# Tied tiles, later remainders, a regrouped conditioning and one root at the end of a decoder step

## The chip, the cores and the metric

The kernel runs on one core of a Trainium2 chip. The metric is the device time of one execution in microseconds (us), the median of the runs. TensorE (PE) multiplies, VectorE (DVE), ScalarE (ACT) and GpSimd (POOL) work on elements, and SyncE (SP) issues most transfers.

## The reference

One layer of a decoder, for a prompt of 512 tokens and a group of 8 sample tokens with their states, at width 1024, in float32:

```
mod = silu(c) @ w_mod + b_mod                  # six parts: shift, scale, gate, twice
h   = rmsnorm(x) * (1 + scale1) + shift1
u   = h @ w_in                                 # 8 column blocks of 1024
o_a = HGRN2 heads of (q, f, i, gate)           # 8 heads, chunked recurrence
o_b = RG-LRU(conv(x_b)) * gelu(y_b)
merged = sigmoid(g_a) * (o_a @ w_branch_a) + sigmoid(g_b) * (o_b @ w_branch_b)
x   = x + gate1 * (merged @ w_out)
h2  = rmsnorm(x) * (1 + scale2) + shift2
x   = x + gate2 * (square(relu(h2 @ w_ff1)) @ w_ff2)
y   = rmsnorm(x) * final_norm_g
```

The outputs are `y_prompt` (512 x 1024), `y_sample` (8 x 1024) and the states after the step.

## The kernel before

Activations lie transposed: 128 features on the partitions, 512 + 8 tokens along the free axis, cut into two halves of 260. Every float32 operand is split in two (a rounded part `whi` or `hi`, and the remainder `wlo` or `lo`), and a product is three matrix products: `whi` x `hi`, `whi` x `lo`, `wlo` x `hi`. A plain tile (`gemm`) makes 128 output features out of 1024: eight blocks k of 128 inputs, three products, two halves, so 48 matmuls. They are issued by `products` (L157), block after block, all three products of a block together.

The weights of a tile are loaded by SP into one of four buffers, the pool `wst` (L104), cast by ACT to `whi` (L114), and the remainder is made by DVE (`wlo`, L118). There are two places for such pairs in this part of the program, so the cast of a tile begins when the tile two before it is done. The loads stand in the order of `weights`: at most `LOADS` = 3 ahead of the splitting, all on SP's queue, each waiting for its buffer.

A scheduler places the instructions on the engines: it goes by the program's data and by priorities (`urgent` lifts an instruction ahead), unless `behind` ties one instruction after another without a wait. In `gemm`, `after` is such a tie for the `whi` products. Before the change it is set only after a conditioning step (`rows_last`), so products of neighbouring tiles may mix.

The conditioning `mod` is computed in pieces. Of its six parts two are made at the start, the other four as eight steps between other work. A step (`mod`, `mod_rows` L362) is 32 matmuls of four loaded rows of `w_mod`, 512 KB each; these rows go through the same four `wst` buffers, but are used as they are, unsplit, and hold their buffer until the step. Four steps stand among the gate products, one at each of four groups, two in the branch tiles (after b3 and a3, set by `share` and `due`), two after the w_out tiles 1 and 4.

The stages: heads, RG-LRU and first gates up to about 430 us, the second gates (`gate_product`, L916, weights `wgate`) up to 482, the branch tiles b0 to b7 and a0 to a7, w_out, then a feed-forward part with a plan of its own.

At the end, the last two of eight feature blocks of x (blocks 6 and 7) get their last products. `final_pair(2, 1)` transposes blocks 4 and 5 of the last token quarters and the samples: ACT squares the result with a running sum (`fss`), DVE multiplies it by `final_norm_g` into `fx` (rows) and `fxs` (samples; in the trace it is part of the tile `fin`). `last_transposes` does the same for blocks 6 and 7 by a product with `gdiag`, `last_squares` squares their x on ACT (`snap`), `last_sums` adds the squares up over the partitions in PSUM, on top of the reduced `fss` (`part`, from `last_parts`). `last_root` takes the square root (ACT) and the reciprocal (DVE), `row` multiplies one quarter of 128 tokens and sends it off, 768 columns and then 256. Quarters 0 and 1 are done earlier, in `last_half`. From (j = 4) on, PE, ACT and DVE work strictly in the order written (`InOrder`; all these instructions carry line 73).

Of the kernel before, what the change touches and what calls it, by code (L numbers as in the profile page):

```python
# [32 lines left out]
LOADS = 3  # L33
MODK = 7
ROWN = 4
FIRSTS = 3
# [44 lines left out]
class Kernel:  # L81
# [67 lines left out]

    def products(self, ps, w, a, first, last, extra=0, halves=(0, 1), after=None):  # L150

        (wh, wl), (ah, al) = w, a
        ps = ps if isinstance(ps, list) else [ps[:, 0], ps[:, 1]]
        for n, (x, y) in enumerate(((wh, ah), (wh, al), (wl, ah))):
            for s in halves:
                c = slice(s * HALF, (s + 1) * HALF + s * extra)
                self.last_product = self.nc.tensor.matmul(ps[s][:, :c.stop - c.start], x, y[:, c],  # L157
                                                          start=first and n == 0, stop=last and n == 2)
# [1266 lines left out]
    def final_pair(self, m, s):  # L1425
# [27 lines left out]
    def added_last(self, j, ps):  # L1453
# [10 lines left out]
        def add_samples(t, op=OP.add):  # L1464
            self.nc.vector.tensor_tensor(zs[t], zs[t], ps[:, n:], op)
# [5 lines left out]
        with self.urgent():  # L1471
# [21 lines left out]
            if j == 3:  # L1493
                self.last_rows = [self.pmm.tile([128, 2, 512], F32, name="mm")[:, 0],
                                  self.pps.tile([128, 512], F32, name="ps")]
                self.last_transposes(1, 1)
                self.last_sums(1, 1)
                add(0, g[0], True)
                add_samples(0)
                samples_done(self.nc.vector, 0)  # L1500
                self.last_squares(1, 0)
                self.last_sums(1, 0)
                self.last_transposes(1, 0)
                sq = self.sm.tile([128, 2, NB], F32, name="sqx")
                for t in (0, 1):
                    self.nc.vector.tensor_tensor(sq[:, t], x[t][:, L:], x[t][:, L:], OP.mult)
                self.last_root(self.fr[:, 2:4], self.sums[:, 1, :2])
                pt = self.ppt.tile([128, 512], F32, name="pt")
                for t in (0, 1):
# [5 lines left out]
                for t in (0, 1):  # L1515
                    self.nc.tensor.matmul(ss, sq[:, t], self.one, start=False, stop=True, skip_group_check=True)
                self.row(2, self.nc.vector)
                self.row(3, self.nc.scalar)
                self.row(2, self.nc.vector, self.last_rows[0])
                r = self.fr[:NB, NC:NC + 1]  # L1520
                self.last_root(r, ss)
                self.row(3, self.nc.scalar, self.last_rows[1])
                self.nc.vector.tensor_scalar(self.fxs[:, :768], self.fxs[:, :768], r, None, OP.mult)
                self.nc.vector.tensor_scalar(self.fxs[:, 768:], pt[:NB, :256], r, None, OP.mult)
                self.nc.scalar.dma_start(self.o["y_s"][:, 0], self.fxs)

    def last_half(self):

        with self.urgent():
# [8 lines left out]
            self.final_pair(2, 1)  # L1538
            self.last_parts(1)

# [15 lines left out]
    def last_sums(self, s, j):  # L1556

        ps = self.sums[:, s, :2]
        first = (s, 1 - j) not in self.summed
        self.summed.add((s, j))  # L1560
        if first:
            self.nc.tensor.matmul(ps, self.ident, self.part[:, 2 * s:2 * s + 2], start=True, stop=True,
                                  skip_group_check=True)
# [7 lines left out]

    def row(self, t, eng, p=None):

# [5 lines left out]
        else:  # L1579
            eng.tensor_scalar(y, src, r, None, OP.mult)  # L1580
        self.nc.sync.dma_start(self.o["y_p"][0, t * 128:(t + 1) * 128, c], y)

    def run(self):
# [508 lines left out]
```

## Time and profile before

| what | value |
|---|---|
| median of 3 runs | 1001.22 us (1001.22 to 1002.68) |
| profiled execution | 1001.28 us, its span 999.5 us |
| busy: PE, DVE, ACT, POOL | 98%, 69%, 52%, 14% of the span |
| matmuls | 9644 |
| granted clock of TensorE, mean | 0.996 |
| transferred | 143.67 MB |

The profile comes from one execution of the span given, 1.8 us shorter than the time of that run. The word that stands behind `<-` in a row of the timeline is what released the instruction, with the idle time of the engine ahead of it. Times in rows are microseconds from the start of the span.

### The profile page before, as it was taken

The page shows a single profiled execution, that of the slowest core. Times are in us where ns is not written, and L with a number is a line of the kernel's source. Part 1 is how long each engine was busy: PE and PEld are TensorE (multiplying, and loading weights), DVE is VectorE, ACT ScalarE, POOL GpSimd, SP SyncE. Part 2 cuts the span into 40 slices and gives each one's busy share as a digit, 9 for nine tenths or more (in the row PEclk, how much of TensorE's full clock was granted, in tenths as well). Part 3 has the DMA queues.
Part 4 walks back from the last instruction along what each step waited for, and adds up shares of the span by engine and source line. Part 5 has one row for each costly group of instructions (what it writes and reads, how often), then busy time and mean ns, then how long its engine had stood idle before and what let it go on. Part 6 is the DMA issues. An engine that isn't in the chain of part 4 may idle for free. (4 is left out here: it accounts for less than half of the span.)

```text
span 999.5 us, 23206 instructions
## 1 busy us (share of the span) xinstructions
PE 981.9 (98%) x9644; PEld 955.6 (96%) x9644; DVE 691.1 (69%) x1359; ACT 523.9 (52%) x996; POOL 135.1 (14%) x247
## 2 busy tenths in 40 slices
PE   8999999999999999999999999999999999999997
PEld 6899999999999999999889999999999999999996
DVE  7795866686596667887525557767677766768785
ACT  5565645735664572565412324566456555646663
POOL 1300000000000100121000000012311331232050
PEclk9999999999999999999999999999999999999998
DMA  9663253253334336357545646322752572272242
GB/s 348 238 200 122 95 166 125 81 170 108 111 117 137 127 100 210 112 183 272 192 159 183 209 161 222 116 83 61 190 147 69 112 191 79 71 185 62 64 85 86
DMA packets 48858, 143.67 MB, mean 144 GB/s; under 512 B 6241, under 2 KB 15905, under 8 KB 47721
## 3 DMA queue, kind: packets, MB, share of 16 engines
q1 hardware_dynamic: 37280, 123.47, 36.8%
q0 software_dynamic: 11456, 18.70, 8.5%
q8 instruction: 75, 1.23, 0.5%
q14 instruction: 31, 0.25, 0.1%
q10 hardware_dynamic: 16, 0.03, 0.0%
HBM read 123.65 MB, written 11.26 MB: 135 GB/s over the span
## 5 line engine op out<-in xcount | busy, mean ns | idle before, releaser
L157 PE MATMUL mm<-h,whi 128*128 128x260 f32 (+1 forms) x2720 | 450.8, 285 | 0.0
L157 PEld LDWEIGHTS mm<-h,whi 128*128 128x128 f32 x2720 | 377.7, 189 | 1.3 <-issue 0.2
L157 PE MATMUL mm<-h,wlo 128*128 128x260 f32 x1360 | 280.4, 285 | 0.4 <-DVE wlo L118 0.4
L118 DVE TENSOR_TENSOR wlo<-wst,whi 128x1024 fp32r<-128x1024 f32 x156 | 190.6, 1223 | 127.2 <-ACT whi L114 122.8
L114 ACT CAST whi<-wst 128x1024 fp32r<-128x1024 f32 x156 | 163.3, 1049 | 151.7 <-PE mm L157 101.4
L157 PEld LDWEIGHTS mm<-h,wlo 128*128 128x128 f32 x1360 | 212.8, 189 | 1.5 <-issue 0.6
L1299 POOL TENSOR_TENSOR ft<-ft,fsh 128x8 f32<-128x8 f32 x28 | 18.4, 658 | 209.1 <-DVE ft L1293 209.1
L1307 DVE TENSOR_TENSOR f<-f 128x260 f32<-128x260 f32 x64 | 27.4, 427 | 27.8 <-ACT f L1302 27.1
L1296 ACT ACTIVATE ft<-ft,fsh 128x512 f32<-128x512 f32 (+2 forms) x36 | 24.0, 676 | 36.1 <-DVE ft L1293 36.1
L157 PE MATMUL mm<-b,whi 128*128 128x260 f32 x256 | 41.4, 284 | 0.9 <-ACT whi L114 0.9
L157 PE MATMUL mm<-a,whi 128*128 128x260 f32 x256 | 41.3, 284 | 0.0
L234 POOL TENSOR_SCALAR ss<-ss 128x4 f32<-128x4 f32 x8 | 2.7, 334 | 285.2 <-ACT g L672 285.2
L157 PE MATMUL mm<-oa,whi 128*128 128x260 f32 x256 | 41.2, 283 | 0.0
L157 PEld LDWEIGHTS mm<-b,whi 128*128 128x128 f32 x256 | 35.1, 189 | 1.7 <-ACT whi L114 1.3
L588 DVE TENSOR_TENSOR X<-X,tb 128x512 f32<-128x512 f32 x48 | 31.0, 691 | 7.0 <-PE ps L576 3.7
L157 PEld LDWEIGHTS mm<-a,whi 128*128 128x128 f32 x256 | 35.0, 188 | 0.8 <-PE pt L362 0.4
L157 PEld LDWEIGHTS mm<-oa,whi 128*128 128x128 f32 x256 | 34.9, 188 | 0.4 <-issue 0.4
L1341 POOL DMA_DIRECT2D ma<-snap x28 | 26.4, 956 | 40.6 <-issue 32.3
L1323 POOL DMA_DIRECT2D ma<-snap x28 | 25.9, 926 | 38.5 <-DMA ma<-snap 23.5
L1302 ACT ACTIVATE f<-ft 128x520 f32<-128x520 f32 (+1 forms) x36 | 20.8, 587 | 15.0 <-POOL ft L1300 13.0
L182 ACT ACTIVATE gate<-pb,pa 128x260 f32<-128x260 f32 x32 | 15.5, 483 | 24.5 <-PE pb L720 24.5
L157 PE MATMUL mm<-b,wlo 128*128 128x260 f32 x128 | 25.9, 284 | 0.5 <-DVE wlo L118 0.5
(566 smaller groups left out, 2071.9 us busy)
## 6 DMA issues: line engine op xcount, KB each, us to landing
wst<-in_w_ff_dram SPq DMA_DIRECT2D x64, 512.0 KB, 4.4
wst<-in_w_in_dram SPq DMA_DIRECT2D x56, 512.0 KB, 3.8
wst<-in_w_mod_dram SPq DMA_DIRECT2D x32, 512.0 KB, 6.2
wm<-in_w_piece_dram SPq DMA_DIRECT2D x4, 1024.0 KB
wm<-in_w_rows_dram SPq DMA_DIRECT2D x4, 1024.0 KB, 11.8
st<-in_state_hgrn_dram SPq DMA_DIRECT2D x8, 512.0 KB
vb<-vd SPq DMA_DIRECT2D x8, 512.0 KB, 4.2
out_dram<-st SPq DMA_DIRECT2D x8, 512.0 KB, 3.7
```

The source lines that it names most:

```text
L114: ins = self.nc.scalar.copy(hi, st)
L118: self.nc.vector.tensor_tensor(lo, st, hi.bitcast(F32), OP.subtract)
L157: self.last_product = self.nc.tensor.matmul(ps[s][:, :c.stop - c.start], x, y[:, c], start=first and n == 0, stop=last and n == 2)
L182: ins = self.nc.scalar.activation(out, x, AF.Sigmoid, **kw)
L234: p.tensor_scalar(out, x, n * EPS, None, OP.add)
L588: last = nc.vector.tensor_tensor(half, half, factors(tbs, x, b), OP.mult)
L1296: nc.scalar.activation(t[:, :p], t[:, :p], AF.Relu, bias=sh[:, 0:1])
L1299: eng.tensor_tensor(t[:, p:], t[:, p:], sh[:, 1:9], OP.add)
L1302: nc.scalar.activation(f, self.two(self.ft)[:, a:a + n], AF.Square)
L1307: self.nc.vector.tensor_tensor(f[:, n], f[:, a], f[:, b], op)
L1323: nc.gpsimd.dma_start(x[1][:, b], v[:, :n], accum_op=OP.add)
L1341: nc.gpsimd.dma_start(x[t][:, a], s[p], accum_op=OP.add)
```

## The change

1. `gemm` ties its `whi` products after the product issued last (`self.last_product`) where there is no conditioning step to tie to.
2. `LATE = 4`: a tile first issues the two `whi` products of blocks 0 to 3 (16 matmuls), then their four `wlo` products (8 matmuls), then blocks 4 to 7 as before. The number of matmuls is the same.
3. The copy of the sample values in `head_sample_v` is urgent.
4. The eight conditioning steps stand in other places: three among the gate products (none at the last group), three in the branch tiles (after b4, a1 and a6), two after the w_out tiles 1 and 4.
5. `final_pair` issues DVE's products ahead of ACT's squares.
6. The end is rewritten: the sum of the samples' squares becomes a third column of the last sums, so that one root of 128 x 3 and one reciprocal serve rows and samples; the transposes stand ahead of the sums; the reduction stands behind the last additions; the samples' first 768 columns are multiplied by POOL; the second piece of row 3 leaves on ACT's queue, the samples on SP's; the PSUM tile for `last_rows[0]` comes from another pool.

```diff
+LATE = 4
@@ products
+            if n not in parts:
+                continue
@@ gemm
-        after, self.rows_last = after or self.rows_last, None
+        after, self.rows_last = after or self.rows_last or self.last_product, None
...
-                n = q * KO + k
-                self.products(ps, (hi[:, k], lo[:, k]), acts[n], n == 0, n == len(keys) * KO - 1, extra,
-                              after=after)
+                for j, parts in ((k, (0, 1, 2)),) if k >= LATE else \
+                        ((k, (0, 1)),) + tuple((j, (2,)) for j in range(LATE) if k == LATE - 1):
+                    n = q * KO + j
+                    self.products(ps, (hi[:, j], lo[:, j]), acts[n], n == 0, n == len(keys) * KO - 1, extra,
+                                  after=after, parts=parts)
@@ head_sample_v
-        nc.vector.tensor_copy(vs, ps[:NB, :128])
+        with self.urgent():
+            nc.vector.tensor_copy(vs, ps[:NB, :128])
@@ final_pair
+        if s:
+            nc.vector.tensor_tensor(self.fxs[:, fs], p2[:NB, :256], self.gbc[:NB, fs], OP.mult)
+        nc.vector.tensor_tensor(self.fx[:, 2 * s:2 * s + 2, fs], p.rearrange("p (t f) -> p t f", f=256),
+                                self.gbc[:, None, fs].to_broadcast([128, 2, 256]), OP.mult)
         for t in range(2):
             nc.scalar.activation(junk, p[:, 256 * t:256 * t + 256], AF.Square,
                                  accum_out=self.fss[:, 2 * s + t, m:m + 1])
         if s:
             nc.scalar.activation(junk[:NB], p2[:NB, :256], AF.Square, accum_out=self.fss[:NB, NC, m:m + 1])
-            nc.vector.tensor_tensor(self.fxs[:, fs], p2[:NB, :256], self.gbc[:NB, fs], OP.mult)
-        nc.vector.tensor_tensor(self.fx[:, 2 * s:2 * s + 2, fs], p.rearrange("p (t f) -> p t f", f=256),
-                                self.gbc[:, None, fs].to_broadcast([128, 2, 256]), OP.mult)
@@ added_last, j == 3
-                self.last_rows = [self.pmm.tile([128, 2, 512], F32, name="mm")[:, 0],
+                self.last_rows = [self.ppb.tile([128, 512], F32, name="pb"),
                                   self.pps.tile([128, 512], F32, name="ps")]
                 self.last_transposes(1, 1)
-                self.last_sums(1, 1)
                 add(0, g[0], True)
                 add_samples(0)
+                self.last_parts(1)
                 samples_done(self.nc.vector, 0)
                 self.last_squares(1, 0)
+                sq = ...                                  # the samples' squares, as before
+                self.last_transposes(1, 0)
+                self.last_sums(1, 1)
                 self.last_sums(1, 0)
-                self.last_transposes(1, 0)
-                self.last_root(self.fr[:, 2:4], self.sums[:, 1, :2])
+                for t in (1, 0):
+                    self.nc.tensor.matmul(self.sums[:NB, 1, 2:3], sq[:, t], self.one, start=False, stop=True,
+                                          skip_group_check=True)
                 pt = ...                                  # two products, as before
-                ss = self.sums[:NB, 0, 2:3]
-                self.nc.tensor.matmul(ss, self.ident[:, :NB], self.part[:, NC:NC + 1], start=True, stop=True,
-                                      skip_group_check=True)
-                for t in (0, 1):
-                    self.nc.tensor.matmul(ss, sq[:, t], self.one, start=False, stop=True, skip_group_check=True)
+                self.last_root(self.fr[:, 2:5], self.sums[:, 1, :3])
+                r = self.fr[:NB, NC:NC + 1]
+                self.nc.gpsimd.tensor_tensor(self.fxs[:, :768], self.fxs[:, :768], r.to_broadcast([NB, 768]), OP.mult)
                 self.row(2, self.nc.vector)
                 self.row(3, self.nc.scalar)
                 self.row(2, self.nc.vector, self.last_rows[0])
-                r = self.fr[:NB, NC:NC + 1]
-                self.last_root(r, ss)
-                self.row(3, self.nc.scalar, self.last_rows[1])
-                self.nc.vector.tensor_scalar(self.fxs[:, :768], self.fxs[:, :768], r, None, OP.mult)
+                self.row(3, self.nc.scalar, self.last_rows[1], self.nc.scalar)
                 self.nc.vector.tensor_scalar(self.fxs[:, 768:], pt[:NB, :256], r, None, OP.mult)
-                self.nc.scalar.dma_start(self.o["y_s"][:, 0], self.fxs)
+                self.nc.sync.dma_start(self.o["y_s"][:, 0], self.fxs)
@@ last_sums: slices 2 -> 2 + s, so that the samples' sums are the third column
@@ run
-        share, due = 1 / KO, 0.5
+        share, due = 3 / (2 * KO), 0.2
...
-            if j == 5:
+            if j == 5 and u < n - 1:
                 mod_step(1)
```

Three places in the order of the instructions. First TensorE between the branch tiles b2 and b3, before the change: `mm_6844` is b1, `mm_6903` b2, `mm_6959` b3; the `b_` names are the blocks of the activations.

```order
L157 MATMUL mm_6844<-b_6059,wlo_6725 128x260 x2
L157 MATMUL mm_6903<-b_6017,whi_6791 128x260 x2
L157 MATMUL mm_6903<-b_6018,whi_6791 128x260 x2
L157 MATMUL mm_6959<-b_6017,whi_6847 128x260 x2
L157 MATMUL mm_6959<-b_6018,whi_6847 128x260 x2
L157 MATMUL mm_6959<-b_6017,wlo_6848 128x260 x2
```

The same place after it: `mm_6872` is b2 and `mm_6928` b3.

```order
L160 MATMUL mm_6872<-b_6059,wlo_6761 128x260 x2
L160 MATMUL mm_6928<-b_6017,whi_6816 128x260 x2
L160 MATMUL mm_6928<-b_6018,whi_6816 128x260 x2
L160 MATMUL mm_6928<-b_6023,whi_6816 128x260 x2
L160 MATMUL mm_6928<-b_6024,whi_6816 128x260 x2
L160 MATMUL mm_6928<-b_6029,whi_6816 128x260 x2
L160 MATMUL mm_6928<-b_6030,whi_6816 128x260 x2
L160 MATMUL mm_6928<-b_6035,whi_6816 128x260 x2
L160 MATMUL mm_6928<-b_6036,whi_6816 128x260 x2
L160 MATMUL mm_6928<-b_6017,wlo_6817 128x260 x2
```

Before, b3 begins four products into b2 and takes the place of 25 products before b2 goes on; now b3 begins with b2 complete, and its first remainder stands behind 16 products. No two plain tiles are mixed any more.

Second, SP's queue of loads from the gates on, before and after:

```order
L104 DMA wst<-in_w_mod_dram 128x1024 x16
L104 DMA wst<-in_w_branch_b_dram 128x1024 x5
L104 DMA wst<-in_w_mod_dram 128x1024 x4
L104 DMA wst<-in_w_branch_b_dram 128x1024 x3
L104 DMA wst<-in_w_branch_a_dram 128x1024 x5
L1142 DMA wst<-in_w_ff_dram 128x1024 x4
```
```order
L105 DMA wst<-in_w_mod_dram 128x1024 x12
L105 DMA wst<-in_w_branch_b_dram 128x1024 x6
L105 DMA wst<-in_w_mod_dram 128x1024 x4
L105 DMA wst<-in_w_branch_b_dram 128x1024 x2
L105 DMA wst<-in_w_branch_a_dram 128x1024 x3
L105 DMA wst<-in_w_mod_dram 128x1024 x2
L1148 DMA wst<-in_w_ff_dram 128x1024 x4
L105 DMA wst<-in_w_mod_dram 128x1024 x2
```

Four rows of `w_mod` less stand ahead of the first branch weights, and two groups of four stand among the branch weights instead of one, the second of them around the first feed-forward loads.

Third, DVE at the end, from the last pair on, before and after:

```order
L73 TENSOR_TENSOR fin<-mm,fin 8x256
L73 TENSOR_TENSOR fx<-mm,fin 128x2x256
L73 TENSOR_REDUCE fin<-fss 128x3
L73 SCALAR_TENSOR_TENSOR ma<-ps,ng,ma 128x252
L73 SCALAR_TENSOR_TENSOR ma<-ps,modT,ma 128x252
L73 TENSOR_TENSOR zs<-zs,ps 128x8 x2
L73 SCALAR_TENSOR_TENSOR ma<-ps,modT,ma 128x252
```
```order
L74 TENSOR_TENSOR fin<-mm,fin 8x256
L74 TENSOR_TENSOR fx<-mm,fin 128x2x256
L74 SCALAR_TENSOR_TENSOR ma<-ps,ng,ma 128x252
L74 SCALAR_TENSOR_TENSOR ma<-ps,modT,ma 128x252
L74 TENSOR_TENSOR zs<-zs,ps 128x8 x2
L74 SCALAR_TENSOR_TENSOR ma<-ps,modT,ma 128x252
L74 TENSOR_TENSOR zs<-zs,ps 128x8
L74 TENSOR_REDUCE fin<-fss 128x3
```

The reduction of the squares stood ahead of the three additions to x; it stands behind them now. Before, the two products at the top waited for ACT's squares of the same tile; now they wait for PE alone.

More of the change, by code (lines that the diff above doesn't have):

```diff
@@ L148, in ready_w, with products @@
             self.wnext_split += 1
-    def products(self, ps, w, a, first, last, extra=0, halves=(0, 1), after=None):
+    def products(self, ps, w, a, first, last, extra=0, halves=(0, 1), after=None, parts=(0, 1, 2)):
         (wh, wl), (ah, al) = w, a
@@ L1493, in added_last @@
             if j == 3:
[L1494 removed]
+                self.last_rows = [self.ppb.tile([128, 512], F32, name="pb"),
                                   self.pps.tile([128, 512], F32, name="ps")]
                 self.last_transposes(1, 1)
[L1497 removed]
                 add(0, g[0], True)
                 add_samples(0)
+                self.last_parts(1)
                 samples_done(self.nc.vector, 0)
                 self.last_squares(1, 0)
[L1502 to L1507 removed]
+                sq = self.sm.tile([128, 2, NB], F32, name="sqx")
+                for t in (1, 0):
+                    self.nc.vector.tensor_tensor(sq[:, t], x[t][:, L:], x[t][:, L:], OP.mult)
+                self.last_transposes(1, 0)
+                self.last_sums(1, 1)
+                self.last_sums(1, 0)
+                for t in (1, 0):
+                    self.nc.tensor.matmul(self.sums[:NB, 1, 2:3], sq[:, t], self.one, start=False, stop=True,
+                                          skip_group_check=True)
                 pt = self.ppt.tile([128, 512], F32, name="pt")
[L1509 removed]
+                for t in (1, 0):
                     self.nc.tensor.matmul(pt[:NB, t * 128:(t + 1) * 128], x[t][:, L:], self.gdiag[:, t], start=True,
                                           stop=True)
[L1512 to L1516 removed]
+                self.last_root(self.fr[:, 2:5], self.sums[:, 1, :3])
+                r = self.fr[:NB, NC:NC + 1]
+                self.nc.gpsimd.tensor_tensor(self.fxs[:, :768], self.fxs[:, :768], r.to_broadcast([NB, 768]), OP.mult)
                 self.row(2, self.nc.vector)
@@ L1556, in last_sums @@
     def last_sums(self, s, j):
-        ps = self.sums[:, s, :2]
+        ps = self.sums[:, s, :2 + s]
         first = (s, 1 - j) not in self.summed
@@ L1561, in last_sums @@
         if first:
-            self.nc.tensor.matmul(ps, self.ident, self.part[:, 2 * s:2 * s + 2], start=True, stop=True,
+            self.nc.tensor.matmul(ps, self.ident, self.part[:, 2 * s:2 * s + 2 + s], start=True, stop=True,
                                   skip_group_check=True)
@@ L1570, in last_root, with row @@
         self.nc.vector.reciprocal(r, r)
-    def row(self, t, eng, p=None):
+    def row(self, t, eng, p=None, queue=None):
         c = slice(0, 768) if p is None else slice(768, D)
@@ L1580, in row @@
             eng.tensor_scalar(y, src, r, None, OP.mult)
-        self.nc.sync.dma_start(self.o["y_p"][0, t * 128:(t + 1) * 128, c], y)
+        (queue or self.nc.sync).dma_start(self.o["y_p"][0, t * 128:(t + 1) * 128, c], y)
     def run(self):
```

1 line of the change is left out of this document (removed).

## The prediction

> **What bounds the kernel now.** First the page, then TensorE's waits over the whole span.
>
> ```profile
> span 999.5 us, 23206 instructions
> PE 981.9 (98%) x9644; PEld 955.6 (96%) x9644; DVE 691.1 (69%) x1359; ACT 523.9 (52%) x996; POOL 135.1 (14%) x247
> ```
> ```profile
> PE pt L362 <- DMA wst<-in_w_mod_dram: 1.5, 1, 1.5
> PE mm L73 <- DVE ma L73: 1.2, 1, 1.2
> PE ps L576 <- DVE X L592: 1.0, 2, 0.7
> PE mm L157 <- ACT whi L114: 0.9, 1, 0.9
> PE ps L576 <- DVE X L588: 0.9, 1, 0.9
> PE mm L157 <- DVE wlo L118: 0.9, 2, 0.5
> 615.00:985.00 370.00, 370.00 (x3065) 369.29 (x3058) 268.92 (x444) 214.93 (x393) 87.69 (x148) 1.00 0.42 110
> ```
>
> TensorE is busy 98% of the span, and over the 370 us from 615 to 985 (the last row, of the view by windows; its second number is PE's busy time) it never stops. The change has as many products of each kind as before; what it can win is waits and the tail. The six waits quoted are single events of 0.5 to 1.5 us, and the timeline tells what they cost:
>
> ```profile
> 465.00 1.93 PE L362 MATMUL pt<-wst,cT 128*32 128x256 f32 x32
> 482.61 0.75 PE L157 MATMUL mm<-b,whi 128*128 128x260 f32 x4
> 483.87 0.51 PE L157 MATMUL mm<-b,wlo 128*128 128x260 f32 x2 [0.51 <-DVE wlo L118]
> 494.76 0.40 PE L157 MATMUL mm<-b,wlo 128*128 128x260 f32 x2
> 496.10 0.39 PE L157 MATMUL mm<-b,whi 128*128 128x260 f32 x1 [0.94 <-ACT whi L114]
> 507.81 1.50 PE L362 MATMUL pt<-wst,cT 128*32 128x256 f32 x24
> 511.35 0.75 PE L157 MATMUL mm<-b,whi 128*128 128x260 f32 x4
> 557.56 1.93 PE L362 MATMUL pt<-wst,cT 128*32 128x256 f32 x32
> 559.42 0.75 PE L157 MATMUL mm<-oa,whi 128*128 128x260 f32 x4
> 988.46 0.28 PE L73 MATMUL ps<-ff3l,whi 128*128 128x260 f32 x1
> 988.58 0.28 PE L73 MATMUL ps<-ff3h,wlo 128*128 128x260 f32 x1
> ```
>
> Products follow each other at 988.58 - 988.46 = 0.12 us, though one shows 0.28: a wait costs more than its idle time, since the pipeline drains. Counted from start to start, the product at 483.87 was due at 482.61 + 4 x 0.12 = 483.09 and lost 0.8; the one at 496.10 was due at 495.00 and lost 1.1. A conditioning step without a wait takes 559.42 - 557.56 = 1.86 us, the one at 507.81 took 3.54 to 511.35 and lost 1.7. Of the 0.9 for late remainders (wlo), 0.51 is the one at 483.87; the other, at 119.93, I count with its idle 0.4 alone. The waits at L576 belong to the HGRN2 heads.
>
> **The branch tiles, 482 to 511 us.** Why the three waits there exist:
>
> ```profile
> 477.86 6.31 SPq L104 DMA_DIRECT2D wst<-in_w_branch_b_dram  x5
> 481.51 1.05 ACT L114 CAST whi<-wst 128x1024 fp32r<-128x1024 f32 x1 [1.98 <-DMA wst<-in_w_branch_b_dram]
> 495.00 1.04 ACT L114 CAST whi<-wst 128x1024 fp32r<-128x1024 f32 x1 [1.47 <-PE mm L157]
> 504.92 1.05 ACT L114 CAST whi<-wst 128x1024 fp32r<-128x1024 f32 x1 [8.87 <-PE mm L157]
> 506.00 1.23 DVE L118 TENSOR_TENSOR wlo<-wst,whi 128x1024 fp32r<-128x1024 f32 x1
> 507.25 0.33 SPq L104 DMA_DIRECT2D wst<-in_w_mod_dram  x1
> 510.78 0.64 PE L362 MATMUL pt<-wst,cT 128*32 128x256 f32 x8 [1.48 <-DMA wst<-in_w_mod_dram]
> ```
>
> Wait at 483.87. The fourth conditioning step of the gates holds all four load buffers until 477.8, so the first branch weight is issued at 477.86 and cast at 481.51; its remainder is late. In the change that step is gone, and six branch loads stand right behind the twelfth conditioning row on SP. The step before it, at 465.00, ends 12 us earlier than the one that held them, so the cast waits only for a place of rounded weights, which the 25th of the 28 gate products frees, two products ahead of b0. Gain 0.8. If the cover fails, LATE still moves the need of the first remainder from behind 4 products to behind 16, 12 x 0.12 = 1.44 us, more than the 0.8 that was lost.
>
> Wait at 496.10. Here the scheduler has put 25 products of tile b3 between those of b2; both places of rounded weights are then in use, b3's cast starts at 495.00 when b1's place is free, and PE stands. With the tie b3 starts one whole tile (48 x 0.12 = 5.76 us) after b2, and its cast, from the same release, is done long before. Gain 1.1.
>
> Wait at 510.78. It is the same interleaving's second bill: b2 ends late, so b4's cast waits 8.87 us, to 504.92, its remainder ends at 507.23, and only then the load buffer is free for the fourth conditioning row: issue 507.25, first use 510.78, so 3.53 us at most for the transfer. In order, that row's buffer comes free 507.23 - 504.92 = 2.31 us after the end of the tile two before the step; the row is needed one tile (5.76) and three quarters of a step (1.4) after that end. Slack 5.76 + 1.4 - 2.31 - 3.53 = 1.3 us. Gain 1.7.
>
> New places. The gates keep three steps (as before, without a wait); the sixth and seventh move behind a1 and a6. The step itself costs 1.86 wherever it stands. Behind a1 the release comes 0.4 to 0.9 us later, since DVE and ACT also merge the branches there, and slack falls to 0.4 to 0.9; behind a6 the same. Bounds for each: 0, if the slack holds, and 1.7, the one stall of this kind in the trace. I take 0. The tile behind a step has 1.86 us more for its weights, and w_out's last product, which needs the eighth merged tile, comes 5 us after that tile's end in order. I count nothing for either.
>
> **The start and the heads.** At 119.93 the need moves by 1.44 us against 0.4 lost: gain 0.4. The urgent copy reorders DVE only ahead of about 105 us, and the order of PE's other work between the heads is the same, so their waits stay: 0. (Rival bounds: 1.9 us, both L576 rows gone, and as much more.)
>
> **The tail.** DVE, not PE, sets it:
>
> ```profile
> 986.99 0.38 ACT L73 ACTIVATE fin<-mm 128x256 f32<-128x256 f32 x1
> 988.49 0.41 DVE L73 TENSOR_TENSOR fin<-mm,fin 8x256 f32<-8x256 f32 x1 [1.68 <-ACT fin L73]
> 990.10 0.46 PE L73 MATMUL mm<-fin,ma 128*128 128x128 f32 x2 [1.24 <-DVE ma L73]
> 990.45 0.48 DVE L73 SCALAR_TENSOR_TENSOR ma<-ps,modT,ma 128x252 f32<-128x252 f32 x1
> 992.14 0.26 ACT L73 ACTIVATE fr<-mm,epsc 128x2 f32<-128x2 f32 x1 [0.76 <-PE mm L73]
> 992.63 0.62 DVE L73 TENSOR_SCALAR fx<-fx,fr 128x768 f32<-128x768 f32 x1
> 993.28 2.32 SPq L1581 DMA_DIRECT2D out_dram<-fx  x4
> 995.78 0.57 ACTq L73 DMA_DIRECT2D out_dram<-fin  x1
> ```
>
> DVE idles 1.68 us behind ACT's squares, with the final adds queued behind, and the add at 990.45, which needs the last product (988.58 + 0.28), is 1.5 us late. The change puts DVE's two products first: they start at 988.49 - 1.68 = 986.81 and take about 1.0 us (an estimate: 0.41 and a companion of 512 columns), and that add starts at about 988.95. ACT's squares pay: they start at about 987.85, 0.9 later than at 986.99, last 1.5 (986.99 to 988.49), and two squares for the sums of some 0.4 each follow, to 990.2. Of PE's work, the transposes now stand ahead of the sums and are done by then; eight products of the sums and four of the sample squares come behind, at about 0.1 each. Root at about 991.4 for 992.14: 0.75 us earlier, and the row results (992.63 before, then 991.9) and their DMAs with it.
>
> The sample row then has no root of its own. It leaves when the last of three is done: three row DMAs on SP (about 0.45 us each from 992.5), VectorE's 8x256 piece (about 993.3), and the new product on POOL, from 991.9. Before, it left at 995.78, 3.72 us ahead of the span's end. Its price:
>
> ```profile
> L1958 POOL MEMSET at<- 128x1024 f32 x1 | 1.0, 951 | 0.0
> L73 POOL TENSOR_TENSOR xsr<-xsr,modT 128x64 f32<-128x64 f32 x1 | 0.6, 645 | 0.1
> L1468 POOL TENSOR_TENSOR zs<-zs,modT 128x8 f32<-128x8 f32 x1 | 0.2, 204 | 23.6 <-DVE zs L73 23.6
> ```
>
> Below, the fill of 1024 columns gives 0.951 x 768 / 1024 = 0.7 us. Above, the two tensor products give (645 - 204) / 56 = 7.9 ns per column, 6.1 us for 768. Neither is near; the middle in ratio is 2.1 us, and I take 2. The Trainium skill ("GPSIMD Engine Reference", 3.1 Elementwise) has 4497 ns for a tensor_tensor of 2048 columns, which makes 1.7 us by proportion; no row here shows it. With 2 us the issue comes at 993.9, 1.9 us earlier; but the rows' 1 MB ahead of it moves only by 0.75. So the tail gains between 0.75 and 1.9; I take 1.3.
>
> Sum against the profiled execution (1001.28; the median of three is 1001.22, so the two stand for each other): 0.4 + 0.8 + 1.1 + 1.7 + 1.3 = 5.3 us off, span 994.2, run 996.0.
>
> **Rivals.**
>
> Rows late at the new places. For it: slack of under 1 us behind a1 and a6, with four feed-forward loads between the second and third row on SP at a1. Against: the step behind a3 now waits for nothing (557.56). Half or all of the b4 stall at each, 1.7 to 3.4 us back: about 998.6. Chance 0.17.
>
> POOL long. At 6.1 us the issue comes at 998.0, 2.2 us later than before; 4.0 of gains remain: 1001.28 - 4.0 + 2.2 = 999.5. Chance 0.07.
>
> POOL in VectorE's way. POOL's product and VectorE's row start on the same reciprocal. For it, POOL operations beside VectorE's stretch:
>
> ```profile
> 963.54 1.25 POOL L1353 TENSOR_TENSOR ma<-ma,zs 128x8 f32<-128x8 f32 x1
> ```
>
> against 0.20 alone. If POOL has the port first, the row waits 2 us, to 993.9, its second piece, the sample piece and the DMA follow at 995.6: the tail gains 0.2 and the run ends at 997.1. If VectorE is first, POOL is 0.6 later and little changes. The Trainium skill ("SBUF — State Buffer", Who interferes with whom) has it so: the pair of ports belongs to whoever issues first, and the other blocks for the whole instruction; the stretch from 0.20 to 1.25 agrees, the reverse direction no row here shows. Chance 0.10.
>
> Slower: transfers, not buffers. The slack rests on 3.53 us for one load, but loads in company take longer:
>
> ```profile
> wst<-in_w_branch_b_dram SPq DMA_DIRECT2D x3, 512.0 KB, 7.7
> ```
>
> (that is from issue to landing, the three issued behind the row at 507.25). With L us each, the steps behind b4, a1 and a6 wait L - 4.8, L - 4.4 and L - 4.4. The gains without them are 5.3, so the kernel is no faster from L = 6.3 on and slower by 2 us from L = 7.0; at 7.7 us, 9.5 - 5.3 = 4.2 slower: 1005.5. Against it: three of four rows are issued well before, the fourth alone. Chance 0.05.
>
> No change: DVE, at 69%, passes the won 4 us back as a wait of the next stage. PE's waits above name no such stage after 615. About 1000. Chance 0.05.
>
> **How the numbers follow.** Forecast 0.56, at 996.0, its own range 994.3 to 997.5 (the tail's 0.75 to 1.9 and a few tenths at the waits each way). The range reaches on to the two late cases: 994.2 to 999.2. A measurement of this kernel can tell about 0.2%, 2 us. Faster than 999.2: the forecast, POOL in the way, most of late rows and a part of POOL long, 0.82. Within: the rest of those and no change, 0.12. Slower 0.06.
>
> **What would show it.** Right: no wait of PE over 0.3 us between 480 and 515, no product of one branch tile among another's, the first branch cast over 1 us ahead of its product; DVE's 8x256 product about 986.8, one root about 991.4, the sample's issue about 994, POOL's product of about 2 us. Wrong: a wait at the conditioning product behind b4, a1 or a6; a POOL product over 3 us, or VectorE's row starting after it; waits between 190 and 375 that differ from before.

## The result and the profile after

The changed kernel takes 999.2 us (median of ten runs, 997.78 to 1001.0) against 1001.15 us: the ratio is 0.998 with a 95% interval of 0.9972 to 0.9989. It is faster, by 2.0 us and not by 5.3.

The profiled execution of the changed kernel is its slowest, 1001.0 us, so its span of 999.0 us is not set against the span of before as a whole. Three stretches are compared instead, taken from the two traces: the start up to the first plain product, the middle from there to the start of the last product, and the tail from there to the end of the span.

| kernel | start | middle | tail |
|---|---|---|---|
| before | 45.94 | 942.64 | 10.91 |
| changed | 46.19 | 941.79 | 10.98 |

The start is the same work in both; over all fourteen traces of this study it lies between 45.03 and 46.26, mostly by one wait for `w_piece` near 23 us, which eleven of them have. The change gained 0.85 us in the middle in this execution and nothing in the tail.

TensorE's waits in the changed kernel (the view by releaser, whole span; us in total, times, longest):

```profile
PE mm L160 <- ACT a L217: 1.0, 1, 1.0
PE ps L582 <- DVE X L598: 1.0, 2, 0.7
PE mm L160 <- ACT whi L115: 0.9, 1, 0.9
PE ps L582 <- DVE X L594: 0.9, 1, 0.9
PE ps L577 <- DVE hlast L780: 0.8, 1, 0.8
PE mm L160 <- DVE X L467: 0.7, 1, 0.7
```

The wait of 1.5 us for a row of `w_mod` is gone, and so is the late remainder of b0. The 0.9 for `whi` has stayed as it was. New are 1.0 for `a` (L217), the input of w_out, and 0.7 for `X` (L467). The waits of the heads (L582) are unchanged, as forecast.

**Branch tile b2.** Timeline of ACT and TensorE in the changed kernel:

```profile
485.72 1.05 ACT L115 CAST whi<-wst 128x1024 fp32r<-128x1024 f32 x1
491.48 1.04 ACT L115 CAST whi<-wst 128x1024 fp32r<-128x1024 f32 x1
491.23 0.40 PE L160 MATMUL mm<-b,wlo 128*128 128x260 f32 x2
492.57 0.63 PE L160 MATMUL mm<-b,whi 128*128 128x260 f32 x3 [0.94 <-ACT whi L115]
```

Two weights are cast here, one when b0 ends (485.7) and one when b1 ends (491.4); in ACT's order the first is b3's and the second b2's: by its semaphores the cast at 485.72 waits for the fourth load of `w_branch_b` and that at 491.48 for the third, as in the kernel before at 489.20 and 495.00. So b2, which is due at 491.47, has to wait until 492.57, 1.1 us, exactly what it lost before at 496.10. The tiles are in order on TensorE, and the wait is there all the same.

**w_out 0.** The step behind a6 runs from 572.42 to 574.3. SP, ACT, DVE and TensorE behind it:

```profile
573.12 1.28 SPq L105 DMA_DIRECT2D wst<-in_w_out_dram  x3
581.32 2.00 ACT L115 CAST whi<-wst 128x1024 fp32r<-128x1024 f32 x2 [3.52 <-DMA wst<-in_w_out_dram]
582.41 1.23 DVE L119 TENSOR_TENSOR wlo<-wst,whi 128x1024 fp32r<-128x1024 f32 x1 [3.35 <-ACT whi L115]
583.55 0.69 DVE L954 TENSOR_TENSOR gp<-mm,gp 128x520 f32<-128x520 f32 x1
586.83 0.51 PE L160 MATMUL mm<-a,whi 128*128 128x260 f32 x2 [1.05 <-ACT a L217]
```

The step holds all four load buffers, so w_out's first three loads are issued at 573.12 and after. The second is on the chip at 577.94, but its cast also waits for TensorE, and in ACT's order the cast of the third stands ahead of it, the same reversal as at b2. The third is on the chip only at 581.30, and its cast starts at 581.32. DVE has its remainder (L119) ahead of a7's product (L954) in its order, idles 3.35 us for it, and begins the product at 583.55 though a7's matmuls ended at about 580.3. Merging and splitting then take until the last block of w_out 0 is due and past it: from start to start that costs 1.2 us, and 0.4 more for the remainder of the same block.

**The tail.** The rows that answer to those of before:

```profile
986.14 0.40 DVE L74 TENSOR_TENSOR fin<-mm,fin 8x256 f32<-8x256 f32 x1
987.23 0.39 ACT L74 ACTIVATE fin<-mm 128x256 f32<-128x256 f32 x1 [0.72 <-DVE fx L74]
987.98 0.28 PE L74 MATMUL ps<-ff3h,wlo 128*128 128x260 f32 x1
988.30 0.48 DVE L74 SCALAR_TENSOR_TENSOR ma<-ps,modT,ma 128x252 f32<-128x252 f32 x1 [0.24 <-PE ps L74]
990.77 0.27 ACT L74 ACTIVATE fr<-mm,epsc 128x3 f32<-128x3 f32 x1 [1.45 <-PE mm L74]
991.28 0.62 DVE L74 TENSOR_SCALAR fx<-fx,fr 128x768 f32<-128x768 f32 x1
991.39 1.83 POOL L1524 TENSOR_TENSOR fin<-fin,fr 8x768 f32<-8x768 f32 x1 [2.84 <-DVE fr L74]
993.37 1.03 SPq L1530 DMA_DIRECT2D out_dram<-fin  x1
```

From the last product on, the root comes after 990.77 - 987.98 = 2.79 us instead of 3.56, and the samples' issue after 5.39 instead of 7.20. POOL's product took 1.83 us. All of that is as forecast, and yet the end comes after 10.98 us instead of 10.91. The chain of waits that ended last says where to look; its last pieces are

```profile
991.28 0.02 POOLq L1524
991.30 0.07 issue
991.36 1.86 POOLq L2079
```

where before it ended with DVE's product for the samples:

```profile
994.75 0.61 DVE fin L73
995.36 0.39 DVEq L2075
```

L2079 (L2075 before) is the end of the program. POOL's records there hold a drain, behind which the engines meet:

| kernel | POOL's last operation ends | its drain ends | SP is through with its transfers | span ends |
|---|---|---|---|---|
| before | 990.98 | 995.92 | 998.72 | 999.49 |
| changed | 993.22 | 998.17 | 997.17 | 998.95 |

The drain ends 4.95 us after POOL's last operation in both. Before, SP was later; in the changed kernel SP is through 1.0 us ahead of it, and the meeting waits for POOL.

A second loss stands ahead of that. The samples now leave on SP's queue, behind the rows, and their last piece lands 3.34 us after the issue, where on ACT's queue it took 2.48 (the issue itself 1.03 for 0.57). So the tail adds up: 1.81 from the earlier issue, less 0.86 for the longer transfer, less 1.02 for POOL, is -0.07.

### The profile page after: what moved, and what is told of

Same layout as the page of the kernel before. It is cut to its first block, busy times and chain, and to the rows that moved or that the text cites. A ratio compares the mean times of both kernels' runs of the same rounds, so it can differ in the third digit from the quotient of the medians.

```text
span 999.0 us, 23200 instructions
## 1 busy us (share of the span) xinstructions
PE 980.8 (98%) x9642; PEld 954.6 (96%) x9642; DVE 690.1 (69%) x1357; ACT 524.2 (52%) x995; POOL 137.4 (14%) x248
## 4 chain that ended last, share of the span: by engine, by line
PE 81%; issue 6%; DVE 4%; DMA 4%; ACT 3%; POOL 1%; SPq 0%; POOLq 0%; ACTq 0%; DVEq 0%
PE mm L160 55%; PE ps L1210 9%; PE pt L1210 4%; PE pb L1210 2%; PE pb L726 1%; PE ps L74 1%; PE mm L74 1%; DMA wm<-in_w_piece_dram 1%; PE ps L582 1%; DMA xT<-in_xT_dram 1%; PE pt L74 1%; DVE wlo L119 1%; PE pt L367 1%; DMA wst<-in_w_out_dram 1%; PE pt L657 1%
## 5 line engine op out<-in xcount | busy, mean ns | idle before, releaser
L160 PE MATMUL mm<-h,whi 128*128 128x260 f32 (+1 forms) x2720 | 427.0, 285 | 0.7 <-DVE X L467 0.7
L160 PEld LDWEIGHTS mm<-h,whi 128*128 128x128 f32 x2720 | 368.1, 188 | 2.1 <-PE mm L160 0.8
L119 DVE TENSOR_TENSOR wlo<-wst,whi 128x1024 fp32r<-128x1024 f32 x156 | 190.6, 1222 | 132.2 <-ACT whi L115 123.5
L160 PE MATMUL mm<-h,wlo 128*128 128x260 f32 x1360 | 254.8, 285 | 0.0
L160 PEld LDWEIGHTS mm<-h,wlo 128*128 128x128 f32 x1360 | 201.8, 189 | 0.8 <-issue 0.6
L160 PE MATMUL mm<-a,whi 128*128 128x260 f32 x256 | 37.9, 284 | 1.3 <-ACT a L217 1.0
L160 PE MATMUL mm<-b,whi 128*128 128x260 f32 x256 | 37.4, 283 | 0.9 <-ACT whi L115 0.9
L160 PE MATMUL mm<-oa,whi 128*128 128x260 f32 x256 | 37.4, 283 | 0.0
L1232 ACT ACTIVATE snap<-ps,ng 128x260 f32<-128x260 f32 (+1 forms) x29 | 13.8, 475 | 21.7 <-PE ps L1210 19.3
```

The costliest lines, as they stand in the source:

```text
L119: self.nc.vector.tensor_tensor(lo, st, hi.bitcast(F32), OP.subtract)
```

## The experiments

Theories after the result. **Place**: `end_gates` steps the counter of the places for rounded weights once (`self.nsplit += 1`); that falls between b1 and b2, so b2 is given b1's place and b3 b0's. Its rival is the one of the prediction, that the mixing of tiles is the cause. **Drain**: POOL's late product holds up the end. Its rival: the samples' transfer sets it. **Step**: the third conditioning step among the branch tiles, close to w_out, costs what its place wins. Its rival: the tie itself makes w_out 0 wait.

### POOL's product back on VectorE

```diff
-  self.nc.gpsimd.tensor_tensor(self.fxs[:, :768], self.fxs[:, :768], r.to_broadcast([NB, 768]), OP.mult)
   ...
+  self.nc.vector.tensor_scalar(self.fxs[:, :768], self.fxs[:, :768], r, None, OP.mult)
   self.nc.vector.tensor_scalar(self.fxs[:, 768:], pt[:NB, :256], r, None, OP.mult)
```

> The changed kernel with one edit: the samples' first 768 columns are multiplied by VectorE again (with the one root), not by GpSimd. Theory (GpSimd closes late: its closing drain ended 4.95 us after its last operation in both traces, 993.22 to 998.17 in the changed kernel, and the program's end waited for it, while SyncE was through at 997.17): from the last reciprocal to the end of the span 7.9 us become 6.9, about 1.0 us less run time than the changed kernel. Rival (the samples' transfer sets the end): the issue moves by at most 0.2 us from 993.37 and the end stays, 7.9 us after the reciprocal.

The ratio to before is 0.9973 (0.9962 to 0.9985), 998.66 us. In the trace:

```profile
989.45 0.18 DVE L74 RECIPROCAL fr<-fr 128x3 f32<-128x3 f32 x1 [1.61 <-ACT fr L74]
990.59 0.60 DVE L74 TENSOR_SCALAR fin<-fin,fr 8x768 f32<-8x768 f32 x1
991.75 1.02 SPq L1530 DMA_DIRECT2D out_dram<-fin  x1
```

The span ends at 996.34, 6.9 us after the reciprocal instead of 7.9; POOL's drain ended at 991.88. The samples' issue comes 2.30 us after the reciprocal, as in the changed kernel (993.37 - 991.07), so the transfer was not what set the end in the changed kernel. Here SP is the last again: it is through at 995.56, 3.7 us behind POOL's drain. Yet the end follows the issue by 4.59 us instead of the 3.71 of before, since the samples again land 3.36 us after their issue. The tail is 9.98 us. The timing alone does not part the two kernels, their intervals overlap; the traces do.

### A tiny late operation on POOL, in the kernel before

```diff
+  self.nc.gpsimd.tensor_tensor(self.fr[:NB, 6:7], r, r, OP.mult)
   self.nc.scalar.dma_start(self.o["y_s"][:, 0], self.fxs)
```

> The kernel before with one added operation: GpSimd squares 8 values (8x1) once the second reciprocal at the end is there; its result is used nowhere. Theory (GpSimd's closing drain takes 4.95 us from its last operation): the operation runs at about 994.75, the drain ends at about 999.8 where SyncE is through at 998.7, so the span ends 1.1 us later. Rival (only the length of a GpSimd operation counts): 0.2 us beside other work, no change.

```profile
994.55 0.18 POOL L1525 TENSOR_TENSOR fr<-fr 8x1 f32<-8x1 f32 x1 [3.66 <-DVE fr L73]
```

The operation ends at 994.73, the drain at 999.68, again 4.95 us later, and the tail grows from 10.91 to 11.99 us. The ratio, 1.0004 (0.9995 to 1.0013), neither shows 1.1 us nor rules it out. With the run above it shows that it is the moment of POOL's last operation that counts, not its length.

### The place counter left alone

In the changed kernel, and in the kernel before without anything of the change:

```diff
 def end_gates(self):
-    self.nsplit += 1
```

> The changed kernel without the extra step of the place counter at the end of the gates (nsplit += 1). Theory (that step gives branch tile b2 the place of b1 instead of b0's, so b2's cast can only start when b1 ends, although PE needs it then): b2's cast starts at b0's end, the wait of 1.1 us at b2's first product goes, about 1.1 us less; the wait of 1.6 us in w_out 0 stays. Rival (the wait has another cause, as the interleaved tiles that the prediction named, or the load): it stays at 1.1.

> The kernel before with that one line taken out, no tie, nothing else of the change. Theory (place counter): b2 and b3 are no longer mixed, since b3's place is no longer free ahead of b2's; the waits of 1.1 us at b2 and of 1.7 us at the first conditioning row of the branch tiles both go: 2.8 us less than before. Rival (the missing tie is the cause): b3's products stand among b2's as before and both waits stay, no change.

TensorE's waits from 475 to 640 us, first the changed kernel's, then that of the kernel before, both without the line:

```profile
PE pt L367 <- DMA wst<-in_w_mod_dram: 3.1, 2, 2.8
```
```profile
PE pt L362 <- DMA wst<-in_w_mod_dram: 2.6, 1, 2.6
PE mm L157 <- DVE wlo L118: 0.5, 1, 0.5
```

The wait for `whi` at b2 is gone in both. In the kernel before, b2 and b3 are also no longer mixed, without any tie, and the wait at the first conditioning row of the branch tiles has gone with it: the mixing was the scheduler's answer to b3's place being free before b2's. But the wait for a row of `w_mod` in these lists is new. It stands at 591.8, in the step behind w_out 1 (about 3 us from start to start), because the line also sets the places from w_out on, and without it that part is shifted too (the next run bears this out). It costs more than its length: within 2 us behind it TensorE's granted clock falls to 0.50 for 3.41 us in both traces, here in the changed kernel's (the view by windows, the 0.50 is the clock),

```profile
596.57:599.98 3.41, 3.41 (x19) 3.41 (x18) 2.42 (x2) 2.24 (x3) 0.00 (x0) 0.50 1.01 372
```

and products start 0.22 us apart there instead of 0.12, which is about 1.5 us more (an estimate: 3.41 x 0.10 / 0.22). So both are no faster: 1.0 (0.9989 to 1.001) and 1.0007 (0.9997 to 1.0017), with middles of 943.52 and 944.06. The theory of the wait at b2 held, and the expected time did not.

A second expectation failed and tells more. The wait of 1.6 us at w_out 0 was to stay in the changed kernel, and it is gone, though the step still stands behind a6. The casts of w_out are in the order of the loads here, and DVE has a7's product ahead of the next remainder:

```profile
579.00 0.70 DVE L954 TENSOR_TENSOR gp<-mm,gp 128x520 f32<-128x520 f32 x1 [1.33 <-PE mm L160]
580.36 1.22 DVE L119 TENSOR_TENSOR wlo<-wst,whi 128x1024 fp32r<-128x1024 f32 x1
```

So the places have a part in the wait at w_out 0 too, through the order of the casts.

### The counter's step moved to w_out

```diff
 def end_gates(self):
-    self.nsplit += 1
 def begin_strassen(self):
+    self.nsplit += 1
```

> The changed kernel with the extra step of the place counter moved from the end of the gates to the begin of w_out's four places, so that w_out on gets its places as in the changed kernel. Theory (without that line at all the two waits of the branch tiles went, but w_out's conditioning waited 3 us, since the places from w_out on were shifted): the 1.1 us at b2 go, nothing new at w_out; 1.1 us less than the changed kernel. Rival (a free b2 pulls the later loads together, whatever the places in w_out): a new wait of 1 us or more in w_out.

The ratio is 0.9972 (0.9961 to 0.9983), 998.58 us. All that is left of waits between 475 and 640 us is

```profile
PE pt L367 <- DMA wst<-in_w_mod_dram: 0.2, 1, 0.2
```

the row behind a1 (0.4 from start to start). The middle is 939.52 us, 2.3 less than in the changed kernel: 1.1 is b2, and 1.6 is that w_out's third load was there at 578.94, early enough; a wait of 0.5 at 228 that only this trace has goes off again. That load landed 5.45 us after its issue, and 5.48 in the run of all edits together, but 6.7 to 7.3 in the other traces with the same steps: whether the counter's move brings this or the execution stays open.

### The tie alone, in the kernel before

```diff
-        after, self.rows_last = after or self.rows_last, None
+        after, self.rows_last = after or self.rows_last or self.last_product, None
```

> The kernel before with the tie of plain tiles alone. The prediction: both waits, of 1.1 us at b2 and of 1.7 us at the conditioning row behind it, go, 2.8 us less than before. The place theory: b2 still waits 1.1 us for b1's place, only the mixing goes and with it the 1.7: 1.7 us less, w_out 0 without a wait above 0.5.

The ratio is 0.9997 (0.9988 to 1.0007).

```profile
PE mm L157 <- DVE wlo L118: 1.4, 2, 0.8
PE mm L157 <- ACT whi L114: 0.9, 1, 0.9
```

The wait for `whi` at b2 stays, as the place theory has it, and the 1.7 us at the conditioning row behind b3 are gone. But the tie has uncovered another wait: b2's remainder, ready 1.2 us after its rounded part, makes TensorE wait at 496.5 for another 1.0 us. Before, b3's products stood there. The middle is 942.28 us, only 0.4 better.

### The changed kernel without the late remainders

```diff
-LATE = 4
+LATE = 0
```

> The changed kernel with LATE = 0: each block's remainder product right behind its two others, as before; all else as changed. Theory: b0's first remainder is ready anyway, since its weights are loaded 12 us earlier; at b2 the remainder of the weights comes about 1.0 us after the rounded part (as with the tie alone) and costs 1.0 us more; the wait of 0.8 us near 125 turns into 0.5 near 119: 0.7 us more than the changed kernel in all. Rival (LATE costs as much at 125 as it wins): no difference above 0.3.

The ratio is 1.0 (0.9992 to 1.0009), 1001.44 us: without LATE nothing is left of the gain. The middle is 943.20, 1.4 us more than in the changed kernel, and 1.0 of it is b2's remainder:

```profile
PE mm L160 <- ACT whi L115: 1.1, 1, 1.1
PE mm L160 <- DVE wlo L119: 0.8, 1, 0.8
```

Near 120 us the wait of 0.8 at 125.6 turns back into one of 0.56 at 119.2: there LATE loses 0.25. The timing (0.998 against 1.0 of before) differs by more than the 0.7 expected and the 1.4 of the trace; the rest is not explained.

### Other places for the conditioning steps

```diff
-            due = mod_step(due + share)
+            if tiles.index((g, m)) in (3, 7, 11):
+                mod_step(1)
```

> The changed kernel with the three conditioning steps of the branch tiles behind b3, b7 and a3 instead of b4, a1 and a6; all else as changed. Theory (the step behind a6 holds the four load buffers until 573, so w_out's first weights come late, DVE waits for their remainders with a7's merge queued behind, and w_out 0 waits 1.2 to 1.6 us for its last block): that wait goes, and the 0 to 0.3 at the step behind a1 too; 1.2 to 1.9 us less than the changed kernel, if the steps behind b3 and b7 do not wait for rows. Rival (the tie makes w_out 0 wait, whatever stands ahead, since before its products were mixed with w_out 1's): the wait at w_out 0 stays above 1 us.

The wait at w_out 0 is gone, and it was not the tie that made it. But the ratio is 0.9981 (0.9972 to 0.999), as of the changed kernel, for a new wait of the same size has come:

```profile
PE mm L160 <- ACT whi L115: 2.2, 2, 1.1
```

One of the two is b2's, the other stands at 536.6 and costs 1.3: a1's weights, which are loaded behind the rows of the step behind b7 and together with feed-forward loads.

### a7's merge ahead of w_out's remainders

```diff
 merge, for m = 7:
-        self.nc.vector.tensor_tensor(s, s, t1, OP.add)
+        added = self.nc.vector.tensor_tensor(s, s, t1, OP.add)
+        self.behind(self.last_lo, added)     # and the later remainders in the same way
```

> The changed kernel with the remainders of w_out 1 and 2 tied behind a7's merge on VectorE (no wait added, only the order); all else as changed. Theory (the wait at w_out 0 comes from VectorE's order: the remainder of w_out 1 stands ahead of a7's product and waits for a load that the step behind a6 holds up): the wait of 0.8 to 1.6 us at w_out 0's last block goes, whenever that load lands; about 1.2 us less than the changed kernel. Rival (only the landing counts, the order is a symptom): a wait of its kind moves to w_out 1's remainder, no gain.

The ratio is 0.9973 (0.9964 to 0.9983), 998.81 us. On DVE:

```profile
580.02 0.70 DVE L956 TENSOR_TENSOR gp<-mm,gp 128x520 f32<-128x520 f32 x1 [1.37 <-PE mm L162]
580.78 0.69 DVE L960 TENSOR_TENSOR gp<-gp,ma 128x520 f32<-128x520 f32 x1
581.80 2.36 DVE L119 TENSOR_TENSOR wlo<-wst,whi 128x1024 fp32r<-128x1024 f32 x2 [0.32 <-ACT whi L115]
```

The third load is late again (6.98 us from its issue to its landing at 580.69, and its remainder, the first of the two at 581.80, waits for its cast), but a7's product no longer stands behind it. Between 475 and 640 us TensorE waits only for b2's weights and 0.3 us for the row behind a1. The middle is 940.03, 1.8 us less than in the changed kernel. As with the counter moved, the interval of the ratio overlaps with the changed kernel's (0.9972 to 0.9989), so the gain is read from the traces.

### All of it together

VectorE's product, the counter moved, the merge ahead, the conditioning as changed:

> The changed kernel with the samples' product on VectorE, the place counter's step moved to w_out, and the remainders tied behind a7's merge; conditioning as changed. Theory: 1.0 + 1.1 + 1.2 = 3.3 us less than the changed kernel, near 995.9; left in the branch tiles is 0.3 to 0.6 for the row behind a1. Rival: the loads of w_out come late and w_out 1 waits instead, near 997.

The ratio to before is 0.9956 (0.9943 to 0.9969), 996.98 us, 4.6 us less than the kernel before and the fastest of all; this interval lies wholly below that of the changed kernel. Between 475 and 640 us no wait is listed any more (the row behind a1 still costs 0.25 from start to start); the middle is 938.72 and the tail 9.98.

Two more combinations fall behind it in the median. With the steps behind b3, b7 and a3, the counter moved and VectorE's product:

> The changed kernel with all three: samples' product on VectorE, the counter moved, conditioning behind b3, b7 and a3. Theory: the gains add, 1.0 + 1.1 + 1.6 = 3.7 us less than the changed kernel, near 995.5. Rival (they share a cover, or the b tiles' rows come late in tight order): under 2 us less.

it is 0.9961 (0.9948 to 0.9973), 997.56 us, with the wait of 1.2 at a1. The three gains do not add, since one is given back. With the fastest kernel's edits and the middle step behind a0:

> The same with the middle conditioning step behind a0 instead of a1, so that its four rows stand ahead of the first feed-forward loads on SyncE. Theory: the row's wait of 0.3 to 0.6 us goes, 0.4 us less than the kernel with the step behind a1. Rival (four feed-forward loads then delay a1's or a2's weights, as with the step behind b7, where a1 waited 1.2 to 1.3): 0.5 to 1 us more.

it is 0.9991 (0.9981 to 1.0), 1000.34 us:

```profile
PE pt L369 <- DMA wst<-in_w_mod_dram: 2.8, 1, 2.8
```
```profile
532.00 1.75 SPq L1153 DMA_DIRECT2D wst<-in_w_ff_dram  x4
534.06 0.33 SPq L105 DMA_DIRECT2D wst<-in_w_mod_dram  x1
```

The fourth row did not come ahead of the feed-forward loads on SP but right behind four of them, and TensorE waited about 3 us for it. As with the waits at 591.8, the granted clock is 0.50 for 3.41 us around the end of this one, from 541.60. The profiled execution took 1004.52 us, and its trace also holds two waits, at 317 and 455, that others do not have; they are not the edit's place. Neither theory had that right.

## Why the prediction was wrong

**Right.** b0's remainder: gone, 0.8. The wait for the conditioning row: gone, 1.7. The waits of the heads: unchanged. The tail up to the issue of the samples: root 0.77 us nearer to the last product (0.75 forecast), the issue 1.8 nearer (1.9), POOL's product 1.83 us (2.0 forecast). The Trainium skill ("GPSIMD Engine Reference", 3.1 Elementwise) gave an estimate of 1.7 by proportion, and the run agrees within 8%. The rival of POOL in VectorE's way did not come: VectorE's row beside it took 0.62 us, as alone. The rule that the first to issue blocks the other (the Trainium skill, "SBUF — State Buffer", Who interferes with whom) is tested by that on one side only: the row was first by 0.1 us and was not slowed, and whether POOL's 1.83 holds a block no row shows.

**b2, 1.1 us: the step failed at its cause.** "Here the scheduler has put 25 products of tile b3 between those of b2; both places of rounded weights are then in use, b3's cast starts at 495.00 when b1's place is free, and PE stands." The cast at 495.00 was b2's own. I had read the names of the tiles off the order of the casts, and that order was not the order of the tiles. The mixing was a result: b2 got the place that comes free last, b3 the one that comes free first, and the scheduler put b3's products where b2 had none. Taking the line out of the kernel before removed wait and mixing together; the tie alone left the wait, and added one of 1.0 that the mixing had hidden.

**The tail, 1.3 us: the step failed at what ends the program.** The sum let the end follow either the samples' issue, by 3.72 us as before, or the rows' transfers, and took 1.3 between the two. In the changed kernel neither set the end. POOL's closing drain, 4.95 us behind its last operation, was in the trace of before as well (990.98 to 995.92, hidden by 2.8 us), and the POOL operation was costed only by its length. The rival "POOL long" asked how long the operation takes, from 6 us on; 2 us were already too many. POOL's late end cost 1.0 us. The 3.72 itself did not hold either: moving the samples from ACT's queue to SP's was given no price, and it made their transfer 0.86 us longer in the changed kernel's trace (0.8 to 0.9 in the traces with VectorE's product). With the product on VectorE the tail gains 0.93 us, inside the forecast's 0.75 to 1.9.

**The new places, 0 taken, bounds 0 to 1.7 each: the value was mis-sized and the mechanism another.** Behind a1 the row's wait was 0.3 us in the changed kernel's trace and 0 to 0.5 in the other traces with that step, near the slack that the sum gave. Behind a6 no row waited; "the tile behind a step has 1.86 us more for its weights" left out that w_out's loads are also held up, and that ACT and DVE have the third one's cast and remainder ahead of a7's merge. Moving the step, leaving the counter's step out, and turning DVE's order each removed the wait. It cost 1.6 us, and 1.2 in the trace with VectorE's product. The prediction itself asked what is queued behind a waiting instruction on DVE only in the tail, not here.

**The start, 0.4 us: mis-sized.** The wait at 119 went, and one of 0.8 came at 125.6 where 0.15 had been: 0.1 us lost.

Together, of 5.3 us: 1.1 at b2, 1.3 in the tail, 1.9 at the new places and 0.5 near 120 did not come. That leaves 0.5, which is what the two traces show (0.85 in the middle less 0.07 in the tail, less 0.25 of start). The medians show 2.0 us. The profiled execution took 1001.0, 1.8 us more than the median; the start (45.0 to 46.3) and the wait at w_out 0, which hangs on the landing of a load (0 to 1.6 in the traces with that step), vary by that much, but no trace of a median execution was taken, so how the 1.5 us divide stays open.

The 1.7 at the conditioning row came by the order of the tiles, as forecast, but the tie alone paid for it with 1.0 at b2's remainder, which LATE then hides: the prediction gave LATE no part in the branch tiles beyond b0.

## What to carry to other kernels

When a tile waits for its weights, ask which place its weights go to and who left it, tile by tile with numbered names, before a mixed order is blamed: it may be the scheduler's answer to the wait. When work is moved to an engine that was idle, count its closing at the end of the program too, not only its duration; and when a transfer moves to another queue, price it on that queue. A wait of TensorE of 3 us can cost more than 3 us: look at the granted clock behind it. And a conditioning step that shares the load buffers can cost something up to two tiles further on: behind a1, behind a6, behind b7 and behind a0 it was another transfer or another engine's queue each time.

## What the runs showed of the hardware

GpSimd's drain at the end of the program ended 4.95 us after its last operation whether that was a product of 128x8 (0.2 us), of 8x1 (0.18) or of 8x768 (1.83); in the kernel before it is hidden. Why it takes that long no run shows.

Between the start and the last products, three of the fourteen traces hold a stretch in which TensorE's granted clock is 0.50: 3.41 us each time, from 596.57 (changed kernel without the counter's step), 595.19 (kernel before without it) and 541.60 (the step behind a0). Each begins near the end of a wait of 2.6 to 2.8 us for a row of `w_mod`, from 0.4 us ahead of it to 1.4 us behind. No other wait there is over 1.6 us in any trace, and none has such a stretch; where the limit lies no run shows.

The samples' transfer (8 rows of 4 KB) landed 2.5 to 2.7 us after its issue on ACT's queue (four traces) and 3.3 to 3.4 us after it on SP's queue (ten traces). The issue itself took 0.6 and 1.0 us; what the rest comes from no run shows.
